# Three tiles multiplied while x comes in, first weight pieces from two queues, and state additions issued later than their products

## The chip, the cores and the metric

The kernel runs on one core of a Trainium2 chip. The metric is device time in microseconds, from the first to the last instruction of the core with what the launch adds around it; lower is better.

## What is computed

One inference step of a hybrid layer, in float32: 256 prompt tokens and 8 x 8 sample tokens (320 columns, T) share the weights. One input projection (2048 to 13344 columns) feeds a Mamba-2 SSD mixer and a gated short convolution, and one output projection takes both. The reference, cut:

```python
h = rmsnorm(x, norm_w)
proj = jnp.einsum('bld,de->ble', h, w_in)
z_s, xbc, dt_raw, z_c, b_c, c_c, v_c = jnp.split(proj, SPLIT_POINTS, axis=-1)
xbc, buf_ssd_new = causal_dwconv(xbc, buf_ssd, conv_ssd_w)      # width 4
xbc = jax.nn.silu(xbc + conv_ssd_b)
xs, bm, cm = jnp.split(xbc, (D_SSM, D_SSM + SSD_GN), axis=-1)
dt = jax.nn.softplus(dt_raw + dt_bias)
y_s, h_new = ssd_scan(xs, dt, -jnp.exp(a_log), bm, cm, d_skip, h_ssm)  # h_new = h * decay + B (dt x)
y_s = grouped_rmsnorm(y_s * jax.nn.silu(z_s), ssd_norm_w, SSD_GROUPS)
conv_out, buf_short_new = causal_dwconv(c_c * v_c, buf_short, conv_short_w)
y_c = b_c * conv_out * jax.nn.silu(z_c)
y = jnp.einsum('ble,ed->bld', jnp.concatenate([y_s, y_c], axis=-1), w_out)
return x + y, h_new, buf_ssd_new, buf_short_new
```

The 8 samples each carry an SSD state of 32 heads x 64 x 128 in and out.

## The kernel before

The input projection is cut into tiles of 128 output columns; `schedule()` lists them: B, C, dt, four x and four z tiles of SSD group 0, four tiles of the short convolution, then the same for groups 1 to 3, then the other short convolutions. A tile is 16 pieces of 128 x 128 weights (k = 0 to 15) against `x`, which lies with its 2048 features over 16 pieces of 128 partitions x 320 columns. To keep float32 accuracy at the faster fp32r rate, weights and x are split: ScalarE casts a quarter tile (`wh`, L145), VectorE subtracts for the rest (`wl`, L146), and each piece takes three products, L165 to L167 (L245 to L247 for the first two tiles). The dt tile has its rest in spare columns and takes two (L161, L162). x is scaled by the norm weight and split the same way into `xh` (ScalarE, L235) and `xl` (VectorE, L236). The row norm itself is computed beside the first products and multiplied in behind the projection (`rb`, L307): it needs the squares of x (L239 on POOL for three quarters, L241 on ScalarE for the last), their sums (L250, L251) and two small groups of products (`rstd`, L260 and L277).

Weights come on SyncE's queue (SP, L132) into three buffers of half a tile; `wh` and `wl` have six buffers of a quarter each, so the split of the next tile runs up to one and a half tiles ahead of the products. Tiles 0 and 1 are multiplied piece by piece as x arrives; tile 2 (dt) follows from its own loads, with `rstd` advanced between its pieces, and tiles 3 onward run in the loop at L691. There, `advance(1)` at three pieces of each tile (`TICKS`) lets a generator issue its next step: `decays()` first (the steps of dt, `laT`, `tr1` and so on), then `ssd_group(g)` for each group. A step ends at a `yield`.

Of `ssd_group`, the change touches the samples' states (L539 to L562). For q = 0 and 1, four states `ht` (b = 2j + q) are multiplied with C (`py`, L542), the four updates `up` come from eight products (L548), POOL multiplies each state with its decay (L552), VectorE adds the update (L554), and POOL stores the state (L555). Behind that come the decay matrices `R` (loaded at L461, steps at L585, exp at L588, product with CBm at L589) and `CE` (L577 on ScalarE, L578 on POOL).

The code's order is not the order on the engines: a scheduler in the framework places each instruction by its own estimate. The order below is read from the built kernels.

Of the kernel before, what the change touches and what calls it, by code (L numbers as in the profile page):

```python
# [84 lines left out]
def hymba_step(ctx: ExitStack, tc: tile.TileContext, A, O):  # L85
# [34 lines left out]
    def load(i):  # L120
# [12 lines left out]
            got.append(r)  # L133
        raws[i] = got

    def split_quarter(i, q):
# [2 lines left out]
        if i < nin and tiles[i][0] == "dt":

            S.copy(h, r)
            V.tensor_sub(h[:, :, H:2 * H], r[:, :, H:2 * H], h[:, :, H:2 * H].bitcast(F32))
            return h, None
# [4 lines left out]

    def split(i):
        if i >= NTILE or i in splits:  # L150
            return
        load(i)
        splits[i] = [split_quarter(i, q) for q in range(KT // KQ)]

    def product(ps, i, hi, lo, start=True, stop=True, tick=None, ticks=TICKS):
        for k in range(KT):
            if tick and k in ticks:
                tick()
            h, l = splits[i][k // KQ]
            if l is None:  # L160
                PE.matmul(ps, h[:, k % KQ, :], hi(k), start=k == 0, stop=False)  # L161
                PE.matmul(ps, h[:, k % KQ, :], lo(k), start=False, stop=k == KT - 1)  # L162
                continue
# [63 lines left out]
    ps0 = [psj.tile([P, T], F32, name=f"pj{i}", tag="pj") for i in range(2)]  # L227
    for q in range(KT // KQ):
        ks = slice(q * KQ, (q + 1) * KQ)
        wq = []  # L230
        for i in range(2):
            wq.append(split_quarter(i, q))
        for k in range(q * KQ, (q + 1) * KQ):
            nwk = vec[:, V_NW + k:V_NW + k + 1]
            S.activation(xh[:, k, :], xr[:, k, :], AF.Copy, scale=nwk)  # L235
            V.scalar_tensor_tensor(out=xl[:, k, :], in0=xr[:, k, :], scalar=nwk,  # L236
                                   in1=xh[:, k, :].bitcast(F32), op0=ALU.mult, op1=ALU.subtract)
        if q < 3:
            GP.tensor_tensor(out=sqx[q], in0=xr[:, ks, :], in1=xr[:, ks, :], op=ALU.mult)  # L239
        else:  # L240
            S.activation(sqx[q], xr[:, ks, :], AF.Square)  # L241
        for k in range(q * KQ, (q + 1) * KQ):
            for i in range(2):
                h, l = wq[i][0][:, k % KQ, :], wq[i][1][:, k % KQ, :]
                PE.matmul(ps0[i], h, xh[:, k, :], start=k == 0, stop=False)  # L245
                PE.matmul(ps0[i], l, xh[:, k, :], start=False, stop=False)  # L246
                PE.matmul(ps0[i], h, xl[:, k, :], start=False, stop=k == KT - 1)  # L247
    acc = sqx[0]
    for q in range(1, 4):
        V.tensor_tensor(out=acc, in0=acc, in1=sqx[q], op=ALU.add)  # L250
# [27 lines left out]
        out.append(p2[:, :T])  # L278

    def inproj(i):  # L280
        if tiles[i][0] == "dt":
            ps = pss.tile([P, 512], F32, name="pdt", tag="py", bufs=1)[:, :T]
        else:
            ps = psj.tile([P, T], F32, name=f"pj{i}", tag="pj")
# [589 lines left out]
```

## Time and profile before

| | us |
|---|---|
| median of 3 runs | 1061.34 (1057.29 to 1063.15) |
| the profiled execution | 1064.92 |
| its span, first to last instruction | 1063.1 |
| TensorE busy in it | 1032.8 |
| VectorE, ScalarE, POOL busy in it | 667.2, 484.5, 193.3 |

Times in the profile are us from the span's start. PE is TensorE's products, PEld its weight loads, DVE VectorE, ACT ScalarE, POOL GpSimd, SP SyncE; L12 is line 12 of the kernel, and a line may be that of a helper, so that L146 is every rest of a split. A product's duration contains its way through the array, so the distance of two starts is its cost in a row of products. The granted clock is the share of TensorE's full 2.4 GHz; its two levels read as 1.00 and 0.50. The profile prints 1.00 from the start of the span, also where products are spaced as at the low level.

### The profile page before, as it was taken

The page shows a single profiled execution, that of the slowest core. Times are in us where ns is not written, and L with a number is a line of the kernel's source. Part 1 is how long each engine was busy: PE and PEld are TensorE (multiplying, and loading weights), DVE is VectorE, ACT ScalarE, POOL GpSimd, SP SyncE. Part 2 cuts the span into 40 slices and gives each one's busy share as a digit, 9 for nine tenths or more (in the row PEclk, how much of TensorE's full clock was granted, in tenths as well). Part 3 has the DMA queues.
Part 4 walks back from the last instruction along what each step waited for, and adds up shares of the span by engine and source line. Part 5 has one row for each costly group of instructions (what it writes and reads, how often), then busy time and mean ns, then how long its engine had stood idle before and what let it go on. Part 6 is the DMA issues. An engine that isn't in the chain of part 4 may idle for free.

```text
span 1063.1 us, 18415 instructions
## 1 busy us (share of the span) xinstructions
PE 1032.8 (97%) x7110; PEld 1006.8 (95%) x7110; DVE 667.2 (63%) x1202; ACT 484.5 (46%) x850; POOL 193.3 (18%) x276
## 2 busy tenths in 40 slices
PE   6999999999999999999999999999999999999995
PEld 5989899989998999889999999999999999999994
DVE  7776878688867976697555555555555644444443
ACT  6663456435654455355444344444444544444440
POOL 3322422062104411342111111111111000000000
PEclk8999999999999999999999999999999999999997
DMA  7446645575448545754745545454545445454542
GB/s 265 145 140 219 199 138 159 163 244 186 141 139 278 178 141 170 253 183 154 244 144 154 149 149 154 145 158 142 156 144 160 146 152 152 146 155 144 157 120 99
DMA packets 64119, 177.18 MB, mean 167 GB/s; under 512 B 10672, under 2 KB 19888, under 8 KB 63904
## 3 DMA queue, kind: packets, MB, share of 16 engines
q1 hardware_dynamic: 60848, 166.04, 50.2%
q0 software_dynamic: 3040, 9.96, 2.5%
q8 instruction: 55, 0.90, 0.4%
q14 instruction: 32, 0.26, 0.1%
q10 hardware_dynamic: 144, 0.01, 0.0%
HBM read 163.41 MB, written 12.58 MB: 166 GB/s over the span
## 4 chain that ended last, share of the span: by engine, by line
PE 89%; DVE 5%; DMA 3%; issue 1%; ACT 1%; POOL 0%; SPq 0%; DVEq 0%; ACTq 0%; POOLq 0%
PE pj L165 21%; PE pj L166 21%; PE pj L167 20%; PE po L167 7%; PE po L165 7%; PE po L166 7%; DVE wl L146 2%; DMA wr<-in_w_in 1%; PE pd L601 1%; DVE ht L554 1%; PE st L528 1%; DVE res L784 1%; DMA xr<-in_x 1%; DMA R<-acd 0%; PE pj L246 0%
## 5 line engine op out<-in xcount | busy, mean ns | idle before, releaser
L146 DVE TENSOR_TENSOR wl<-wr,wh 128x512 fp32r<-128x512 f32 x544 | 386.8, 716 | 299.4 <-ACT wh L145 295.2
L145 ACT CAST wh<-wr 128x512 fp32r<-128x512 f32 x544 | 333.0, 619 | 460.2 <-PE pj L167 309.1
L165 PE MATMUL pj<-xh,wh 128*128 128x320 f32 x1632 | 513.0, 314 | 0.0
L166 PE MATMUL pj<-xh,wl 128*128 128x320 f32 x1632 | 505.2, 310 | 6.6 <-DVE wl L146 6.6
L167 PE MATMUL pj<-xl,wh 128*128 128x320 f32 x1632 | 504.2, 309 | 0.0
L166 PEld LDWEIGHTS pj<-xh,wl 128*128 128x128 f32 x1632 | 306.8, 188 | 10.3 <-DVE wl L146 7.9
L165 PEld LDWEIGHTS pj<-xh,wh 128*128 128x128 f32 x1632 | 306.7, 188 | 6.4 <-issue 4.8
L167 PEld LDWEIGHTS pj<-xl,wh 128*128 128x128 f32 x1632 | 306.8, 188 | 0.0
L167 PE MATMUL po<-ycl,wh 128*128 128x320 f32 x256 | 79.0, 309 | 0.0
L166 PE MATMUL po<-ysh,wl 128*128 128x320 f32 x256 | 79.0, 309 | 0.0
L166 PE MATMUL po<-ych,wl 128*128 128x320 f32 x256 | 79.0, 309 | 0.0
L165 PE MATMUL po<-ych,wh 128*128 128x320 f32 x256 | 79.0, 309 | 0.0
L165 PE MATMUL po<-ysh,wh 128*128 128x320 f32 x256 | 79.0, 309 | 0.0
L167 PE MATMUL po<-ysl,wh 128*128 128x320 f32 x256 | 79.0, 308 | 0.0
L657 POOL COPY sso<-pad 128x18 f32<-128x18 f32 x16 | 5.1, 316 | 237.2 <-DVE pad L655 237.2
L166 PEld LDWEIGHTS po<-ych,wl 128*128 128x128 f32 x256 | 48.0, 187 | 0.0
L165 PEld LDWEIGHTS po<-ysh,wh 128*128 128x128 f32 x256 | 48.0, 187 | 0.0
L166 PEld LDWEIGHTS po<-ysh,wl 128*128 128x128 f32 x256 | 48.0, 187 | 0.0
L165 PEld LDWEIGHTS po<-ych,wh 128*128 128x128 f32 x256 | 48.0, 187 | 0.0
L167 PEld LDWEIGHTS po<-ycl,wh 128*128 128x128 f32 x256 | 48.0, 187 | 0.0
L167 PEld LDWEIGHTS po<-ysl,wh 128*128 128x128 f32 x256 | 48.0, 187 | 0.0
L765 POOL TENSOR_TENSOR acco<-acco,sqo 128x320 f32<-128x320 f32 x13 | 11.7, 899 | 190.9 <-ACT sqo L764 190.9
(213 smaller groups left out, 847.4 us busy)
## 6 DMA issues: line engine op xcount, KB each, us to landing
wr<-in_w_in SPq DMA_DIRECT2D x206, 512.0 KB, 3.7
wr<-in_w_out SPq DMA_DIRECT2D x64, 512.0 KB, 3.8
ht<-in_h SPq DMA_DIRECT2D x32, 256.0 KB, 5.9
out_hs<-ht POOLq DMA_DIRECT2D x32, 256.0 KB, 4.6
R<-acd SPq DMA_DIRECT2D x20, 256.0 KB, 6.9
res<-in_x SPq DMA_DIRECT2D x1, 2560.0 KB, 9.9
xr<-in_x SPq DMA_DIRECT2D x7, 320.0 KB, 6.3
wr<-in_w_in SPq DMA_DIRECT2D x8, 256.0 KB, 6.2
```

What stands on the lines that cost most here:

```text
L145: S.copy(h, r)
L146: V.tensor_sub(l, r, h.bitcast(F32))
L165: PE.matmul(ps, h, hi(k), start=start and k == 0, stop=False)
L166: PE.matmul(ps, l, hi(k), start=False, stop=False)
L167: PE.matmul(ps, h, lo(k), start=False, stop=stop and k == KT - 1)
L528: PE.matmul(p, Btok[:, c * P:(c + 1) * P], xw, start=True, stop=True)
L554: V.tensor_tensor(out=ht, in0=ht, in1=ups[j], op=ALU.add)
L601: PE.matmul(pd[u * HD:(u + 1) * HD, o:o + n], xdt[c][:, h * HD:(h + 1) * HD], Rs[c, h][0][:, Rs[c, h][1], :], start=True, stop=c != 1)
L657: GP.tensor_copy(sso[:, j], win(pad, TP, (NL + 2, NB + 1), (1, 2)))
L765: GP.tensor_tensor(out=acc, in0=acc, in1=sq, op=ALU.add)
L784: V.tensor_tensor(out=r[:, d, :], in0=r[:, d, :], in1=pr[0], op=ALU.mult)
```

## The change

Start. Tiles 0, 1 and 2 (`NFIRST` = 3, dt among them) are multiplied piece by piece as x arrives. Their first quarter is loaded in pieces of two k instead of four, the first such piece of tiles 0 and 2 from ScalarE's queue, all else from SP. Ten products of a zero tile (`NWARM`) stand ahead of the first real product. The accumulators of the three tiles lie in other PSUM pools than before, all squares of x are ScalarE's, and `rstd` is advanced between the pieces of tile 4 (`NFIRST` + 1). Tiles 3 and 4 are multiplied ahead of the loop and kept in `ahead`; the convolutions of tiles 0, 1, 3 and 4 follow when `rb` is there.

States. In `ssd_group` the loads of the odd states are issued before the `up` products, POOL's four multiplications are issued together, and the additions and stores follow behind a `yield`, two and two with another `yield` between them. The two yields that followed for q = 0 stay. A group thus has three steps more.

The diff, cut to its core:

```diff
-    for q in range(KT // KQ):
-        for k in range(q * KQ, (q + 1) * KQ, 2):
-            if k:
-                SP.dma_start(xr[:, k:k + 2, :], A["x"][:, k:k + 2, :])
-            if k == q * KQ:
-                for i in range(2):
-                    SP.dma_start(raws[i][k // KH][:, k % KH:k % KH + KQ, :], A["w_in"][i, :, k:k + KQ, :])
...
+    xload(0, 1)
     S.dma_start(vec[:, :KT], A["vec"][:, :KT])
+    first(S, 0, 0, 2)
+    first(SP, 1, 0, 2)
+    first(S, 2, 0, 2)
+    xload(1, 1)
+    for i in range(NFIRST):
+        first(SP, i, 2, 2)
+    xload(2, 2)
+    for q in range(1, KT // KQ):
+        for i in range(NFIRST):
+            first(SP, i, q * KQ, KQ)
+        xload(q * KQ, 2)
+        xload(q * KQ + 2, 2)
...
+    psw = psj.tile([P, T], F32, name="pjw", tag="pj")
+    for _ in range(NWARM):
+        PE.matmul(psw[:, :P], warm, warm, start=True, stop=True)
...
+    for q in range(KT // KQ):
+        k0 = q * KQ
+        wq = [wtiles(i, q) for i in range(NFIRST)]
+        n = 2 if q == 0 else KQ
+        for k in range(0, KQ, n):
+            for i in range(NFIRST):
+                if i == 0 and n == 2:
+                    xsplit(k0 + k)
+                split_piece(i, wq[i], k0 + k, n)
+            for m in range(n == 2, n):
+                xsplit(k0 + k + m)
+            for kk in range(k0 + k, k0 + k + n):
+                for i in range(NFIRST):
+                    h, l = wq[i]
+                    PE.matmul(ps0[i], h[:, kk % KQ, :], xh[:, kk, :], start=kk == 0, stop=False)
+                    if l is not None:
+                        PE.matmul(ps0[i], l[:, kk % KQ, :], xh[:, kk, :], start=False, stop=False)
+                    PE.matmul(ps0[i], h[:, kk % KQ, :], xl[:, kk, :], start=False, stop=kk == KT - 1)
+    split(3)
+    load(4)
...
-        if q < 3:
-            GP.tensor_tensor(out=sqx[q], in0=xr[:, ks, :], in1=xr[:, ks, :], op=ALU.mult)
-        else:
-            S.activation(sqx[q], xr[:, ks, :], AF.Square)
...
+    for q in range(4):
+        S.activation(sqx[q], xr[:, q * KQ:(q + 1) * KQ, :], AF.Square)
...
+    ahead = {}
     pr = []
-    gens.append(rstd([acc[:, n, :] for n in range(2)], DM, "rx", pr))
-    pdt = inproj(2)
+    for i in range(NFIRST, NFIRST + 2):
+        load(i + 2)
+        split(i + 1)
+        if i == NFIRST + 1:
+            gens.append(rstd([acc[:, n, :] for n in range(2)], DM, "rx", pr))
+        ahead[i] = inproj(i)
...
+            if q == 0:
+                for b in range(4):
+                    hload(2 * b + 1)
             ups = [sm(f"up{g}_{q}_{j}") for j in range(4)]
...
-                ht = hts.pop(b)
+                ht = hts[b]
                 GP.tensor_tensor(out=heads(ht, g), in0=heads(ht, g),
                                  in1=perhead(dec[:, b * H + HPG * g:b * H + HPG * (g + 1)]), op=ALU.mult)
+            yield
+            for j in range(4):
+                b = 2 * j + q
+                ht = hts.pop(b)
                 V.tensor_tensor(out=ht, in0=ht, in1=ups[j], op=ALU.add)
                 GP.dma_start(O["hs"][g, :, b, :], ht)
+                if j == 1:
+                    yield
             if q == 0:
-                for b in range(4):
-                    hload(2 * b + 1)
-                yield
                 yield
                 yield
```

What stands in a row on the engines, at the places that the prediction speaks of. `wh0_1` is quarter 1 of tile 0, the last number an instance. ScalarE at the second quarter of the first tiles, before:

```order
L235 ACTIVATE xh_75<-xr_80,vec_81 128x320 x4
L145 CAST wh0_1_182<-wr0_0_84 128x512
L145 CAST wh1_1_186<-wr1_0_86 128x512
L235 ACTIVATE xh_75<-xr_80,vec_81 128x320 x4
L145 CAST wh0_2_223<-wr0_1_85 128x512
L145 CAST wh1_2_227<-wr1_1_87 128x512
```

and now:

```order
L253 ACTIVATE xh_75<-xr_80,vec_83 128x320 x2
L144 CAST wh0_1_213<-wr0_0_84 128x512
L285 ACTIVATE sqx0_386<-xr_80 128x1280
L144 CAST wh1_1_215<-wr1_0_86 128x512
L144 CAST wh2_1_217<-wr2_0_88 128x512
L253 ACTIVATE xh_75<-xr_80,vec_83 128x320 x4
L144 CAST wh0_2_264<-wr0_1_85 128x512
L144 CAST wh1_2_266<-wr1_1_87 128x512
L285 ACTIVATE sqx1_387<-xr_80 128x1280
```

There are three casts instead of two for each quarter, and a square of x stands among them. 

VectorE in the second half of the states of group 1, before (`wl26_3` is the last rest of tile 26, `wl27_0` the first of tile 27, `c1` a product of the short convolution):

```order
L146 TENSOR_TENSOR wl26_3_2592<-wr26_1_2462,wh26_3_2591 128x512
L562 TENSOR_TENSOR xdt2_1_2344<-xdt2_1_2344,py1_2517 128x512
L589 TENSOR_TENSOR R2_0_1_2655<-R2_0_1_2655,CBm1_2317 128x512
L554 TENSOR_TENSOR ht1_1_2546<-ht1_1_2546,up1_1_0_2630 128x512
L554 TENSOR_TENSOR ht3_1_2548<-ht3_1_2548,up1_1_1_2631 128x512
L554 TENSOR_TENSOR ht5_1_2550<-ht5_1_2550,up1_1_2_2632 128x512
L554 TENSOR_TENSOR ht7_1_2552<-ht7_1_2552,up1_1_3_2633 128x512
L146 TENSOR_TENSOR wl27_0_2684<-wr27_0_2575,wh27_0_2683 128x512
L647 TENSOR_TENSOR c1_2677<-pj25_2595,rb2_397 128x320
```

and now:

```order
L149 TENSOR_TENSOR wl26_3_2612<-wr26_1_2486,wh26_3_2611 128x512
L633 TENSOR_TENSOR R2_0_1_2750<-R2_0_1_2750,CBm1_2341 128x512
L633 TENSOR_TENSOR R0_0_1_2752<-R0_0_1_2752,CBm1_2341 128x512
L149 TENSOR_TENSOR wl27_0_2695<-wr27_0_2595,wh27_0_2694 128x512
L633 TENSOR_TENSOR R0_1_1_2816<-R0_1_1_2816,CBm1_2341 128x512
L606 TENSOR_TENSOR xdt2_1_2368<-xdt2_1_2368,py1_2541 128x512
L629 TENSOR_SCALAR R1_0_1_2843<-R1_0_1_2843,ac_tok_569 128x128
L599 TENSOR_TENSOR ht1_1_2546<-ht1_1_2546,up1_1_0_2669 128x512
L599 TENSOR_TENSOR ht3_1_2548<-ht3_1_2548,up1_1_1_2670 128x512
L691 TENSOR_TENSOR c1_2688<-pj25_2615,rb2_559 128x320
L149 TENSOR_TENSOR wl27_1_2699<-wr27_0_2595,wh27_1_2698 128x512
L599 TENSOR_TENSOR ht5_1_2550<-ht5_1_2550,up1_1_2_2671 128x512
```

The additions to ht1 and ht3 moved behind `wl27_0`, those to ht5 and ht7 behind `wl27_1`; the R products moved ahead of them.

VectorE in the first half of the same group now:

```order
L149 TENSOR_TENSOR wl25_3_2501<-wr25_1_2384,wh25_3_2500 128x512
L599 TENSOR_TENSOR ht0_1_2443<-ht0_1_2443,up1_0_0_2554 128x512
L599 TENSOR_TENSOR ht2_1_2445<-ht2_1_2445,up1_0_1_2555 128x512
L599 TENSOR_TENSOR ht4_1_2447<-ht4_1_2447,up1_0_2_2556 128x512
L599 TENSOR_TENSOR ht6_1_2449<-ht6_1_2449,up1_0_3_2557 128x512
L149 TENSOR_TENSOR wl26_0_2600<-wr26_0_2484,wh26_0_2599 128x512
```

The same six rows stood there before, in this order.

POOL in the second half of group 1, before:

```order
L578 TENSOR_TENSOR CE0_1_2820<-CE0_1_2820,C1_1841 128x512
L552 TENSOR_TENSOR ht1_1_2546<-ht1_1_2546,dec_408 128x512
L552 TENSOR_TENSOR ht3_1_2548<-ht3_1_2548,dec_408 128x512
L552 TENSOR_TENSOR ht5_1_2550<-ht5_1_2550,dec_408 128x512
L552 TENSOR_TENSOR ht7_1_2552<-ht7_1_2552,dec_408 128x512
L578 TENSOR_TENSOR CE1_1_2844<-CE1_1_2844,C1_1841 128x512
L555 DMA out_hs<-ht1_1_2546 128x512
```

and now:

```order
L622 TENSOR_TENSOR CE0_1_2919<-CE0_1_2919,C1_1858 128x512
L622 TENSOR_TENSOR CE1_1_2943<-CE1_1_2943,C1_1858 128x512
L593 TENSOR_TENSOR ht1_1_2546<-ht1_1_2546,dec_570 128x512
L593 TENSOR_TENSOR ht3_1_2548<-ht3_1_2548,dec_570 128x512
L593 TENSOR_TENSOR ht5_1_2550<-ht5_1_2550,dec_570 128x512
L593 TENSOR_TENSOR ht7_1_2552<-ht7_1_2552,dec_570 128x512
L600 DMA out_hs<-ht1_1_2546 128x512
```

The second CE product moved ahead of the four multiplications. On SP the loads of the odd states keep their place among the weights.

## Rows read from the trace of the kernel before

**Rows 1.** The page, busy time of each engine: us busy, share of the span, instructions.

```profile
PE 1032.8 (97%) x7110; PEld 1006.8 (95%) x7110; DVE 667.2 (63%) x1202; ACT 484.5 (46%) x850; POOL 193.3 (18%) x276
```

**Rows 2.** The table of stretches, all engines; a line gives the stretch and its length, then busy us (and instructions) of PE, PEld, DVE, ACT and POOL, the granted TensorE clock, the DMA share and GB/s.

```profile
0.00:5.57 5.57, 0.00 (x1) 0.01 (x1) 0.57 (x2) 2.71 (x5) 0.44 (x9) 1.00 0.63 162
5.57:18.00 12.43, 8.71 (x29) 6.81 (x29) 11.23 (x10) 10.54 (x22) 7.68 (x3) 0.95 1.01 375
18.00:24.00 6.00, 6.00 (x24) 6.00 (x25) 6.00 (x11) 2.51 (x4) 0.00 (x0) 0.54 0.66 246
...
90.00:130.00 40.00, 37.61 (x243) 33.25 (x243) 30.24 (x61) 15.00 (x26) 17.94 (x20) 0.96 0.72 237
...
200.00:245.00 45.00, 43.29 (x296) 39.19 (x295) 35.64 (x69) 18.10 (x31) 17.81 (x21) 1.00 0.68 223
...
300.00:355.00 55.00, 54.67 (x377) 50.56 (x376) 41.31 (x81) 23.08 (x42) 19.02 (x24) 1.00 0.69 216
...
410.00:470.00 60.00, 57.80 (x398) 53.69 (x398) 44.44 (x84) 25.32 (x47) 19.40 (x26) 1.00 0.64 208
```

**Rows 3.** The timeline of TensorE, from the first product to the first products of tile 3 (37.15); start, us, engine, line, operation, output<-input, in brackets the idle time before it and what ended it.

```profile
5.57 0.64 PE L245 MATMUL pj<-xh,wh 128*128 128x320 f32 x1 [5.57 <-ACT wh L145]
...
12.57 0.47 PE L246 MATMUL pj<-xh,wl 128*128 128x320 f32 x1
12.84 0.47 PE L247 MATMUL pj<-xl,wh 128*128 128x320 f32 x1
...
17.87 0.64 PE L246 MATMUL pj<-xh,wl 128*128 128x320 f32 x1 [2.02 <-DVE wl L146]
...
32.51 1.39 PE L260 MATMUL rxs<-ones,sqx 128*128 128x1 f32 x12
33.76 0.39 PE L161 MATMUL pdt<-xh,wh 128*128 128x320 f32 x1
...
36.19 0.83 PE L277 MATMUL rxb<-con,rxr 128*128 128x128 f32 x6
36.78 0.39 PE L161 MATMUL pdt<-xh,wh 128*128 128x320 f32 x1
...
37.15 0.31 PE L165 MATMUL pj<-xh,wh 128*128 128x320 f32 x1
37.30 0.31 PE L166 MATMUL pj<-xh,wl 128*128 128x320 f32 x1
```

**Rows 4.** The table of stretches of 1 us for TensorE alone, behind the idle spell of group 0: busy us, granted clock, DMA share, GB/s.

```profile
126.00:127.00 1.00, 1.00 (x6) 0.50 1.07 270
129.00:130.00 1.00, 1.00 (x7) 0.86 0.04 8
```

**Rows 5.** The timelines of ScalarE, VectorE and POOL while x comes in, columns as in rows 3.

```profile
8.00 1.92 ACT L235 ACTIVATE xh<-xr,vec 128x320 fp32r<-128x320 f32 x4 [0.24 <-DMA xr<-in_x]
9.82 1.12 ACT L145 CAST wh<-wr 128x512 fp32r<-128x512 f32 x2
...
17.32 1.01 ACT L235 ACTIVATE xh<-xr,vec 128x320 fp32r<-128x320 f32 x2
18.24 1.26 ACT L241 ACTIVATE sqx<-xr 128x1280 f32<-128x1280 f32 x1
...
8.60 5.89 DVE L236 SCALAR_TENSOR_TENSOR xl<-xr,vec,xh 128x320 fp32r<-128x320 f32 x4
...
8.14 2.53 POOL L239 TENSOR_TENSOR sqx<-xr 128x1280 f32<-128x1280 f32 x1 [7.17 <-DMA xr<-in_x]
```

**Rows 6.** The list of DMA issues of the first 20 us: output<-input, queue, count, KB each, median us from issue to landing.

```profile
xr<-in_x SPq DMA_DIRECT2D x7, 320.0 KB, 6.3
wr<-in_w_in SPq DMA_DIRECT2D x8, 256.0 KB, 6.2
...
xr<-in_x SPq DMA_DIRECT2D x2, 160.0 KB, 3.0
```

**Rows 7.** The list of waits, TensorE: who waited for whom, us in total, times, longest.

```profile
PE pj L166 <- DVE wl L146: 6.6, 5, 2.2
...
PE tr L377 <- DVE laT L370: 1.3, 1, 1.3
```

**Rows 8.** The timelines of VectorE and POOL in group 2, behind ScalarE's first CE (341.36), and of TensorE at the wait of group 0 (124.43), columns as in rows 3.

```profile
341.36 2.53 DVE L585 TENSOR_SCALAR R<-R,ac_tok 128x128 f32<-128x128 f32 x3 [0.66 <-ACT CE L577]
343.82 3.00 DVE L146 TENSOR_TENSOR wl<-wr,wh 128x512 fp32r<-128x512 f32 x2
346.74 0.68 DVE L562 TENSOR_TENSOR xdt<-xdt,py 128x512 f32<-128x512 f32 x1
...
348.19 2.47 DVE L554 TENSOR_TENSOR ht<-ht,up 128x512 f32<-128x512 f32 x4
350.58 0.68 DVE L146 TENSOR_TENSOR wl<-wr,wh 128x512 fp32r<-128x512 f32 x1
...
342.77 4.95 POOL L552 TENSOR_TENSOR ht<-ht,dec 128x512 f32<-128x512 f32 x4
...
124.43 0.41 PE L166 MATMUL pj<-xh,wl 128*128 128x320 f32 x1 [2.11 <-DVE wl L146]
```

**Rows 9.** The timeline of VectorE at the first two convolutions, six steps.

```profile
40.71 3.01 DVE L437 SCALAR_TENSOR_TENSOR cv<-pad,vec,cv 128x344 f32<-128x344 f32 x6
```

**Rows 10.** The view of one tile, R, from 100 to 125 us (group 0): duration in ns, min/median/max, first and last start.

```profile
L585 DVE TENSOR_SCALAR R<-R,ac_tok x19: 249/282/1328, 107.5 to 115.9; 128x128 f32<-128x128 f32 x11, 128x64 f32<-128x64 f32 x8
```

More of the change, by code (lines that the diff above doesn't have):

```diff
@@ L69 @@
 TICKS = (5, 10, 15)
+NFIRST = 3
+NWARM = 10
 def schedule():
@@ L134, in load, with split_piece @@
         raws[i] = got
+    def split_piece(i, hl, k, n):
+        r = raws[i][k // KH][:, k % KH:k % KH + n, :]
+        h, l = hl
+        h = h[:, k % KQ:k % KQ + n, :]
+        S.copy(h, r)
+        if l is None:
+            V.tensor_sub(h[:, :, H:2 * H], r[:, :, H:2 * H], h[:, :, H:2 * H].bitcast(F32))
+        else:
+            V.tensor_sub(l[:, k % KQ:k % KQ + n, :], r, h.bitcast(F32))
     def split_quarter(i, q):
-        r = raws[i][q * KQ // KH][:, (q * KQ) % KH:(q * KQ) % KH + KQ, :]
         h = wp.tile([P, KQ, P], F32R, name=f"wh{i}_{q}", tag="wh", bufs=6)
[L139 to L143, printed above, removed]
         l = wp.tile([P, KQ, P], F32R, name=f"wl{i}_{q}", tag="wl", bufs=6)
-        S.copy(h, r)
-        V.tensor_sub(l, r, h.bitcast(F32))
+        split_piece(i, (h, l), q * KQ, KQ)
         return h, l
@@ L159, in product @@
             h, l = splits[i][k // KQ]
[L160 to L163, printed above, removed]
             h, l = h[:, k % KQ, :], l[:, k % KQ, :]
@@ L173, in hymba_step, with first, xload @@
     xr = sp0.tile([P, KT, T], F32, name="xr")
+    warm = sp0.tile([P, P], F32, name="warm")
+    V.memset(warm, 0.0)
     vec = cp.tile([P, NV], F32, name="vec")
-    SP.dma_start(xr[:, :1, :], A["x"][:, :1, :])
-    S.dma_start(vec[:, :KT], A["vec"][:, :KT])
-    for i in range(2):
-        raws[i] = [sp0.tile([P, KH, P], F32, name=f"wr{i}_{hf}") for hf in range(2)]
-    for q in range(KT // KQ):
-        for k in range(q * KQ, (q + 1) * KQ, 2):
-            if k:
-                SP.dma_start(xr[:, k:k + 2, :], A["x"][:, k:k + 2, :])
-            if k == q * KQ:
-                for i in range(2):
-                    SP.dma_start(raws[i][k // KH][:, k % KH:k % KH + KQ, :], A["w_in"][i, :, k:k + KQ, :])
-                    if i == k == 0:
-                        SP.dma_start(xr[:, 1:2, :], A["x"][:, 1:2, :])
-    load(2)
+    for i in range(NFIRST):
+        raws[i] = [sp0.tile([P, KH, P], F32, name=f"wr{i}_{hf}") for hf in range(2)]
+    def first(e, i, k, n):
+        e.dma_start(raws[i][k // KH][:, k % KH:k % KH + n, :], A["w_in"][i, :, k:k + n, :])
+    def xload(k, n):
+        SP.dma_start(xr[:, k:k + n, :], A["x"][:, k:k + n, :])
+    xload(0, 1)
+    S.dma_start(vec[:, :KT], A["vec"][:, :KT])
+    first(S, 0, 0, 2)
[10 more added lines that the diff above has]
+        xload(q * KQ + 2, 2)
     con = cp.tile([P, NC_], F32, name="con")
@@ new lines, in hymba_step, with xsplit @@
+    psw = psj.tile([P, T], F32, name="pjw", tag="pj")
+    for _ in range(NWARM):
+        PE.matmul(psw[:, :P], warm, warm, start=True, stop=True)
+    ps0 = [sm(f"pf{i}")[:, :T] for i in range(2)]
+    ps0.append(pss.tile([P, 512], F32, name="pdt", tag="py", bufs=1)[:, :T])
+    pdt = ps0[2]
+    def xsplit(k):
+        nwk = vec[:, V_NW + k:V_NW + k + 1]
+        S.activation(xh[:, k, :], xr[:, k, :], AF.Copy, scale=nwk)
+        V.scalar_tensor_tensor(out=xl[:, k, :], in0=xr[:, k, :], scalar=nwk,
+                               in1=xh[:, k, :].bitcast(F32), op0=ALU.mult, op1=ALU.subtract)
@@ new lines, in wtiles @@
+    def wtiles(i, q):
+        h = wp.tile([P, KQ, P], F32R, name=f"wh{i}_{q}", tag="wh", bufs=6)
+        if tiles[i][0] == "dt":
+            return h, None
+        return h, wp.tile([P, KQ, P], F32R, name=f"wl{i}_{q}", tag="wl", bufs=6)
+    for q in range(KT // KQ):
[10 more added lines that the diff above has]
+            for kk in range(k0 + k, k0 + k + n):
+                for i in range(NFIRST):
+                    h, l = wq[i]
[3 more added lines that the diff above has]
+                    PE.matmul(ps0[i], h[:, kk % KQ, :], xl[:, kk, :], start=False, stop=kk == KT - 1)
@@ L280, in inproj @@
     def inproj(i):
[L281 to L284, printed above, removed]
+        ps = psj.tile([P, T], F32, name=f"pj{i}", tag="pj")
         product(ps, i, lambda k: xh[:, k, :], lambda k: xl[:, k, :], tick=lambda: advance(1))
@@ L694, in hymba_step @@
             ps = ps0[i]
+        elif i in ahead:
+            ps = ahead.pop(i)
         else:
```

20 lines of the change are left out of this document (removed).

## The prediction

> **What bounds the kernel now.** I read the page's busy table first: TensorE is busy for 1032.8 us of a span of 1063.1 [rows 1]. So an edit is worth only TensorE time without a product, or products at the low clock; the reader is to look for these two and for nothing else. The table of stretches gives the idle time: 5.57 us before the first product, 12.43 - 8.71 = 3.72 us while x comes in, and 2.39, 1.71, 0.33 and 2.20 us in the stretches that hold the four SSD groups [rows 2]. The rest lies at the kernel's end, which the change does not touch. The timeline of TensorE gives the clock. Warm, products of 320 columns start 0.146 us apart (37.15 to 37.30); at 12.57 to 12.84 they are still 0.27 us apart, which is the lower level, 1.2 of 2.4 GHz [rows 3]. From 18 to 24 us only 24 products run, granted 0.54 [rows 2]. Behind the idle spell of group 0 the grant is 0.50 until about 129 us, with 6 products a us [rows 4]. The list of waits names who is late: in the groups the rest of a split weight piece (`wl`) from VectorE, 6.6 us in five waits, and once 1.3 us for `laT` [rows 7].
>
> **First tiles.** Before, tiles 0 and 1 take their 96 products while x comes, and the 32 of dt follow; tile 3 begins at 37.15. In between lie the row-norm products, 33.76 - 32.51 = 1.25 and 36.78 - 36.19 = 0.59 us [rows 3], which now move behind tile 3. The same 128 products thus end at the equivalent of 37.15 - 1.84 = 35.3 us.
> Now for the new end. *Transfers.* Ahead of x pieces 2 and 3 stood 160 + 256 + 160 + 256 KB, with themselves 1152 KB, and ScalarE went on at 8.00 when they had landed [rows 5, 6]. Now it is two times 160, six of 128 and 320 = 1408 KB. The 256 KB more cost 0.7 us at 375 GB/s or 1.6 us at 162 [rows 2]; I take 0.9, so 8.9. *ScalarE.* Its pieces follow each other 0.46 us apart for x (1.92 for four), 0.5 for a cast (1.12 for two), 1.2 for a square [rows 5]. Between the landing and x piece 4 stand two x, three casts and a square, which the order puts there: 0.9 + 1.5 + 1.2, so piece 4 is ready at 13.1. *TensorE.* Behind it are 12 of 16 pieces with 8 products each, 96 x 0.146 = 14.0, hence 27.1. *Who else could be last:* ScalarE has 14 x, 9 casts and 3 squares from 8.9 on, 6.4 + 4.5 + 3.6, and ends at 23.4. VectorE has about as much, now without POOL's squares beside it, with which four x rests took 5.89 us [rows 5]. The last x came at 17.3 [rows 5]; 1 MB more at 375 GB/s makes it 20.1. So TensorE itself is last. I add 0.9 us for spells at the low clock, since it still waits at about 6 to 9 and 11.6 to 13 us: tile 3 begins at 28.0, **a gain of 7.3**. Bounds: without the square in the way 25.9 (9.4 gained). With two spells like that of 18 to 24 us, where 24 products took 6.0 instead of 3.5 us [rows 2, 3], it is 32.1 (3.2 gained).
> The ten warming products read 128 columns. Two row-norm products of this shape start some 0.2 us apart warm [rows 3]; at the low level twice that, 4 us in all, so they end near 5.2 where the first real one starts at 5.57 now. They can hold up only the first pieces, which then wait for x 2 and 3 anyway: nothing. The two pieces on ScalarE's queue I count at nothing too: what they bring early waits likewise.
> **The burst behind.** Four convolutions instead of two now follow the row norm. Between `rb` and the first weight rest of tile 7 VectorE has some 13 us to do: twelve convolution steps alone are 6.0 [rows 9]. TensorE has tiles 5 and 6 to cover it, 96 x 0.146 = 14.0. It fits with 0.9 us to spare; if it does not, the excess is a wait. The wait of 1.3 us for `laT` [rows 7] moves into tile 8 and I leave it as it is, with 1 us to either side.
>
> **State additions.** The first half of each group does not change its place: in the order of VectorE the four additions of ht0, 2, 4 and 6 still stand in one piece. The second half does. Take group 2. From the end of ScalarE's CE at 341.36 VectorE does three R, two `wl`, xdt, R, four additions, and then the first rest of the next tile, ready at 351.2 [rows 8]. An addition is 0.6 us, a rest 0.6 (0.68 with its tail), an R product with CBm 0.65 alone. Now (group 1 in the order, tiles 26 and 27) only two R products stand between `wl26_3` and `wl27_0`, so piece 0 is early by more than the wait. But an R product, xdt, an R step, two additions and c come before `wl27_1`. Counted up to piece 1, the queue holds two R products and a short step more and two additions less: 1.3 + 0.2 - 1.2 = 0.3 us more than before. TensorE needs piece 1 one quarter tile, 12 x 0.146 = 1.75 us, after piece 0. Before, c and a rest, 1.0 us, lay between them. So a wait of w at piece 0 becomes w + 1.0 + 0.3 - 1.75 = w - 0.45 at piece 1. The waits of 2.11 [rows 8], 1.71, 0.33 and 2.20 (group 0 had 0.28 more, earlier) turn into 1.7, 1.25, 0 and 1.75: the work is mostly moved. That is 1.9 us. POOL's multiplications now stand behind CE1, so the two rests at 343.82, 3.00 us beside them [rows 8] where two take 1.3, lose their neighbour and others get it. I take 0.6 us for that. The low spell after group 0 (about 3.4 us, so 1.6 lost [rows 4]) may go with the shorter wait: 0.5. **Gain 3.0**; bounds -1 (a little more contention) and 8.2 (all waits and the spell gone). On POOL the stores queue behind the additions as they did; POOL is busy for 18% [rows 1]. The early odd loads keep their place in SP's order.
>
> **Rivals.** *The clock falls again.* While TensorE waits for x, the grant drops as it did for 18 to 24 us, and two slow spells take 5 us: 3.2 in place of 7.3, so 1056.9. For it: products of 8.9 to 13 us leave gaps. Against it: the longest gap then is about 2 us, and the drop came behind two waits, the second of 2.02 us [rows 3]. The Trainium skill, page "TensorE: Matmul & The Clock Gate", section "What's actually happening", has the low clock as the default that activity releases; by that the ten products help and the gaps hurt, and the trace agrees on both.
> *The group waits go altogether.* If the moved multiplications fall beside operations that read PSUM, VectorE is not stretched: 6.6 + 1.6 instead of 3.0, so 1047.6. For it: beside POOL's work xdt took 0.68 [rows 8]. Against it: the count above.
> *POOL's port, slower.* The moved multiplications stand beside R, R, `wl`, R, which read SBUF twice. In group 2, three R steps (0.28 each by their median [rows 10]) and two rests would take 2.2 alone and took 5.4: a stretch of 3.2 us beside POOL work of 6.3 us. If the whole 6.3 counted in the new place, each group would lose 3.1 more, 12.4 in all, and a wait that long brings the low spell that 2.11 us brought to group 0, 1.6 us in each: 1063.1 - 10.3 + 12.4 + 6.4 = 1071.6. It decides from 10.3 / 4 = 2.6 us of added loss in each group. Against it: the old neighbours read SBUF alone too. The Trainium skill, page "SBUF — State Buffer", section "SBUF: two separate sides", calls the port an exclusive lock for the whole instruction; by it the full stretch would be paid, and the trace shows half.
>
> **The numbers.** The profiled execution took 1064.92 us, the median is 1061.34 (1057.29 to 1063.15). Its products are the same in each run, so a faster run has less waiting to lose; I start from the middle of the two, 1063.1. 1063.1 - 7.3 - 3.0 = 1052.8: **1053 us**. Chances: the forecast (1050 to 1056) 0.55; the clock 0.17; group waits all gone 0.13; both halves bring little (about 1060) 0.10; slower by the port 0.05. A measurement of this kernel tells about 0.5% (5.3 us) from no change, so faster begins below 1056.0: 0.55, 0.13 and part of the clock case, 0.75; the same 0.20; slower 0.05. The range, 1046 to 1059, holds the first three cases.
>
> **What would show it.** Right: first product of tile 3 near 28 us; 0.146 us spacing from 13 us on; no square on POOL; idle of 1 to 2 us before the second piece of tiles 13, 27 and 55 and none before the first. Wrong: tile 3 after 31 us or a grant of 0.5 beyond 15 us (clock); rests of 1.5 us in a row and waits over 3 us in the groups (port); a wait before tile 7 (burst); no waits in the groups.

## The result and the profile after

The changed kernel takes 1047.78 us (median of 4 runs, 1047.37 to 1048.97); the kernel before took 1062.24 (1057.29 to 1064.19) beside it. The ratio is 0.9873, 95% interval 0.9837 to 0.9908: faster by 14.5 us, where 10 were forecast. The time lies in the stated range, but outside the 1050 to 1056 of the likeliest case; it is where the second rival (the group waits go altogether, 1047.6) had put it.

The page, busy time of each engine, against [rows 1]:

```profile
PE 1028.9 (98%) x7130; PEld 1004.4 (96%) x7130; DVE 656.2 (63%) x1206; ACT 486.7 (47%) x856; POOL 188.1 (18%) x273
```

The span is 1045.6 us, 17.5 less than that of the profiled execution before. That execution was slower than its kernel's median (1064.92 us against 1062.24), the one after slightly faster than its own, so 3 of the 17.5 us are scatter between executions; where in the kernel they lie no trace shows. TensorE's busy time fell by 3.9 only, so most of the rest is idle time that is gone. The list of waits, TensorE (who waited for whom, us in total, times, longest), of the changed kernel, against [rows 7]:

```profile
PE pf L277 <- ACT xh L253: 1.3, 2, 0.9
...
PE pjw L245 <- DVE warm L180: 1.1, 1, 1.1
PE pdt L277 <- DVE wh L147: 0.6, 1, 0.6
PE tr L415 <- DVE laT L408: 0.4, 1, 0.4
```

No line for `wl` is left: neither the 3.2 us while x came in nor the 6.6 us of the groups. Where the 17.5 us came from is read from two tiles whose place in the order is the same in both kernels: the transposes `xt`, ahead of the state work in each group, and the output products `po` behind all groups. The view of one tile, first of the kernel before, then of the changed one; the times are the first and the last start:

```profile
L516 PE MATMUL xt<-con,x x32: 271/272/273, 89.1 to 436.4; 128*128 128x128 f32 x32
L165 PE MATMUL po<-ych,wh x256: 307/308/310, 822.2 to 1040.0; 128*128 128x320 f32 x128
```

```profile
L554 PE MATMUL xt<-con,x x32: 270/272/273, 80.3 to 421.0; 128*128 128x128 f32 x32
L169 PE MATMUL po<-ych,wh x256: 310/310/310, 804.5 to 1022.3; 128*128 128x320 f32 x128
```

At the first `xt` the changed kernel is 89.1 - 80.3 = 8.8 us ahead, at the first `po` 822.2 - 804.5 = 17.7. So between these two executions the stretch up to the first `xt` gave 8.8 us and the four groups 8.9. The start itself, timeline of TensorE, against [rows 3]:

```profile
1.06 4.37 PE L245 MATMUL pjw<-warm 128*128 128x128 f32 x20 [1.06 <-DVE warm L180]
5.18 0.54 PE L277 MATMUL pf<-xh,wh 128*128 128x320 f32 x2
5.57 0.31 PE L279 MATMUL pf<-xh,wl 128*128 128x320 f32 x1
5.71 0.31 PE L280 MATMUL pf<-xl,wh 128*128 128x320 f32 x1
...
12.97 0.42 PE L277 MATMUL pf<-xh,wh 128*128 128x320 f32 x1 [0.87 <-ACT xh L253]
...
27.48 0.31 PE L169 MATMUL pj<-xh,wh 128*128 128x320 f32 x1
```

Products in a row are 0.146 us apart (the upper level, 2.4 GHz) from 5.57 on, the last gap is the one before x piece 4, at 12.97, and tile 3 begins at 27.48 where 28.0 was forecast. Group 2, timelines of VectorE and then POOL behind ScalarE's first CE (which ends at about 326.0), against [rows 8]:

```profile
323.27 4.54 DVE L629 TENSOR_SCALAR R<-R,ac_tok 128x64 f32<-128x64 f32 x17
327.74 1.28 DVE L149 TENSOR_TENSOR wl<-wr,wh 128x512 fp32r<-128x512 f32 x2
...
333.62 0.69 DVE L599 TENSOR_TENSOR ht<-ht,up 128x512 f32<-128x512 f32 x1 [0.96 <-POOL ht L593]
334.63 0.69 DVE L599 TENSOR_TENSOR ht<-ht,up 128x512 f32<-128x512 f32 x1 [0.32 <-POOL ht L593]
335.23 0.48 DVE L691 TENSOR_TENSOR c<-pj,rb 128x320 f32<-128x320 f32 x1
335.63 1.52 DVE L149 TENSOR_TENSOR wl<-wr,wh 128x512 fp32r<-128x512 f32 x1
337.07 1.27 DVE L599 TENSOR_TENSOR ht<-ht,up 128x512 f32<-128x512 f32 x2
```

```profile
326.05 1.29 POOL L622 TENSOR_TENSOR CE<-CE,C 128x512 f32<-128x512 f32 x1 [3.18 <-ACT CE L621]
329.69 2.90 POOL L622 TENSOR_TENSOR CE<-CE,C 128x512 f32<-128x512 f32 x1 [2.35 <-ACT CE L621]
332.54 4.06 POOL L593 TENSOR_TENSOR ht<-ht,dec 128x512 f32<-128x512 f32 x4
```

Two rests that took 3.00 us now take 1.28, since POOL's multiplications start at 332.54, behind them. The price stands further down: the additions wait for POOL, 0.96 and 0.32 us, and the rest of piece 1 of tile 41 takes 1.52 beside it. It is ready at 337.07. TensorE starts tile 41 at 335.88 and needs the piece for its 14th product, 335.88 + 13 x 0.146 = 337.78: 0.7 us to spare. Behind the other three groups nothing is to spare. In group 0 the rest of piece 1 of tile 13 starts at 113.15 and ends at 113.15 + 1.52 = 114.67; its product starts at 114.72, 0.33 us behind the one before instead of 0.146. Such a delay is too short to show in the list of waits.

### The profile page after: what moved, and what is told of

Read it like the earlier page. It is cut to its first block, busy times and chain, and to the rows that moved or that the text cites. A ratio compares the mean times of both kernels' runs of the same rounds, so it can differ in the third digit from the quotient of the medians.

```text
span 1045.6 us, 18464 instructions
## 1 busy us (share of the span) xinstructions
PE 1028.9 (98%) x7130; PEld 1004.4 (96%) x7130; DVE 656.2 (63%) x1206; ACT 486.7 (47%) x856; POOL 188.1 (18%) x273
## 4 chain that ended last, share of the span: by engine, by line
PE 95%; DVE 3%; ACT 1%; DMA 1%; issue 0%; DVEq 0%; SPq 0%
PE pj L169 23%; PE pj L170 22%; PE pj L171 22%; PE po L169 7%; PE po L171 7%; PE po L170 7%; PE pd L645 1%; PE py L580 1%; DVE cv L475 1%; PE st L566 1%; DVE res L830 1%; PE up L589 1%; DVE wl L149 0%; DMA xr<-in_x 0%; ACT xh L253 0%
## 5 line engine op out<-in xcount | busy, mean ns | idle before, releaser
L149 DVE TENSOR_TENSOR wl<-wr,wh 128x512 fp32r<-128x512 f32 (+1 forms) x546 | 385.1, 711 | 297.0 <-ACT wh L144 293.3
L144 ACT CAST wh<-wr 128x512 fp32r<-128x512 f32 (+1 forms) x551 | 334.8, 616 | 441.9 <-PE pj L171 282.7
```

The source lines that it names most:

```text
L149: V.tensor_sub(l[:, k % KQ:k % KQ + n, :], r, h.bitcast(F32))
```

## The experiments

Times are medians; "before" is the kernel before, run beside the others, and ratios stand with their 95% interval.

**The two halves by themselves.** `start_only` has the changed start and ssd_group() as before, `groups_only` the other way round.

> The new start with the state updates of the kernel before. Theory (the two halves are independent): tile 3 begins at 27.5 as in the changed kernel, and the group waits come back: about 6 us of idle time for wl, some 9 us on the path with the low clock behind the longest; 1055 to 1058. Rival (the new start alone removes the waits, because VectorE's order in front of the group changes too): under 2 us of waits for wl, 1047 to 1050.

> The start of the kernel before with the new state updates. Theory (independent halves): tile 3 begins at 37.2, no wait for wl in the groups; 1054 to 1057. Rival (the groups gain only with the new start): waits for wl of 3 us or more remain, 1058 to 1062.

Before took 1064.48 us. `start_only`: 1051.94, ratio 0.9889 (0.9863 to 0.9915). `groups_only`: 1057.24, 0.9934 (0.9912 to 0.9956). Alone they gain 12.5 and 7.2 us, 19.8 in sum, against 14.5 for both at once (at a median of 1062.24 us before). Their lists of waits, TensorE, `start_only` first:

```profile
PE pj L170 <- DVE wl L149: 3.3, 3, 1.7
```

```profile
PE pj L166 <- DVE wl L146: 1.5, 3, 0.8
```

With the old state updates and the new start the group waits come back, but only half of them, 3.3 of 6.6 us. Neither expectation had that. With the new updates and the old start 1.5 us are left, between the two expectations as well. So the halves overlap: each takes away part of the same waits. The first starts of `xt` and `po` say how much, since the four groups lie between them:

| kernel | first `xt` | first `po` | between |
|---|---|---|---|
| before | 89.1 | 822.2 | 733.1 |
| before, profiled again | 90.0 | 822.8 | 732.8 |
| start_only | 79.9 | 807.8 | 727.9 |
| groups_only | 88.3 | 814.5 | 726.2 |
| the changed kernel | 80.3 | 804.5 | 724.2 |

The new start alone takes 5.2 us off the groups, the new updates alone 6.9, both together 8.9. On top of the new start the updates are thus worth 3.7 us. The seven profiles of variants of the start further down, with the new updates, have 723.5 to 724.8 between the two tiles.

**POOL's work or the place of the additions?** `no_odd_mult` is `start_only` without POOL's second four multiplications, so it leaves the decay of the odd samples' states out:

```diff
-                GP.tensor_tensor(out=heads(ht, g), in0=heads(ht, g), ...
+                if q == 0:
+                    GP.tensor_tensor(out=heads(ht, g), in0=heads(ht, g), ...
```

> As start_only, with the additions of the second half in one piece at their old place, but POOL's four multiplications of the second half are left out (the odd sequences' states are not decayed). Theory A (what the move took away is POOL's work beside VectorE: the last R steps 3.4 us and the two rests 3.0 us beside it): R steps at 1.8 or less and two rests in 1.3, VectorE 2.3 to 3.3 us earlier in each group, no wait or under 1 us in all; 1047 to 1049. Theory B (of the forecast: what counts is that the additions stand behind a piece of the next tile, POOL's company is worth 0.6 us in all): four additions of 0.6 us stay ahead of the first piece and waits of 4 us or more remain; 1052 to 1056.

1047.07 us, ratio 0.9848 (0.9826 to 0.9871), and no wait for `wl` at all, with all four additions still in one piece ahead of the next tile. Theory A holds. From the first `xt` (80.5) to the first `po` (803.9) it takes 723.4 us, 0.8 less than the changed kernel. Group 2 of `start_only`, VectorE and POOL behind the first CE, and then of `no_odd_mult`:

```profile
326.40 3.44 DVE L623 TENSOR_SCALAR R<-R,ac_tok 128x128 f32<-128x128 f32 x3 [0.25 <-ACT CE L615]
329.76 3.00 DVE L149 TENSOR_TENSOR wl<-wr,wh 128x512 fp32r<-128x512 f32 x2
326.45 1.30 POOL L616 TENSOR_TENSOR CE<-CE,C 128x512 f32<-128x512 f32 x1 [3.32 <-ACT CE L615]
327.70 4.50 POOL L590 TENSOR_TENSOR ht<-ht,dec 128x512 f32<-128x512 f32 x4
```

```profile
322.95 4.44 DVE L624 TENSOR_SCALAR R<-R,ac_tok 128x64 f32<-128x64 f32 x17
327.31 1.28 DVE L149 TENSOR_TENSOR wl<-wr,wh 128x512 fp32r<-128x512 f32 x2
...
325.62 1.28 POOL L617 TENSOR_TENSOR CE<-CE,C 128x512 f32<-128x512 f32 x1 [3.07 <-ACT CE L616]
328.74 1.30 POOL L617 TENSOR_TENSOR CE<-CE,C 128x512 f32<-128x512 f32 x1 [1.83 <-ACT CE L616]
```

In `start_only` five VectorE operations, worth 3 x 0.28 + 2 x 0.6 = 2.0 us alone [rows 8, 10], last from 326.40 to 332.68, about as long as the five POOL operations beside them (326.45 to 332.20). Instruction by instruction they take turns: the three R end at 327.83, 328.84 and 329.84, each 0.08 us behind the end of a POOL operation (327.75, 328.75, 329.76). The Trainium skill, page "SBUF — State Buffer", section "SBUF: two separate sides", has the port as an exclusive lock for a whole instruction; these rows agree, 6.3 us for 2.0.

**Is it enough to come later?** `late_one_piece` is the changed kernel with multiplication and addition in one loop again. The two yields of that loop stand behind the first half instead, so that the second half comes as late as in the changed kernel:

```diff
-            yield
-            for j in range(4):
-                b = 2 * j + q
-                ht = hts.pop(b)
                 V.tensor_tensor(out=ht, in0=ht, in1=ups[j], op=ALU.add)
                 GP.dma_start(O["hs"][g, :, b, :], ht)
-                if j == 1:
-                    yield
             if q == 0:
+                yield
+                yield
```

> As the changed kernel, POOL's second half behind both CE, but the four additions in one piece again, ahead of the second piece of the next tile. In the changed kernel that piece was ready within 0.3 us of its need. Theory (splitting two and two matters, since VectorE waits for POOL's multiplications, one in 1.0 us): the second piece is about 1 us late in each group, 3 to 5 us of waits, 1050 to 1053. Rival (only the later POOL place matters): under 1 us of waits, 1047 to 1049.

1051.53 us, ratio 0.9885 (0.9858 to 0.9913), as slow as `start_only`. The theory holds. Its wait line, and VectorE in group 2:

```profile
PE pj L170 <- DVE wl L149: 4.3, 4, 1.4
```

```profile
335.84 0.69 DVE L595 TENSOR_TENSOR ht<-ht,up 128x512 f32<-128x512 f32 x1 [0.95 <-POOL ht L593]
...
338.85 0.69 DVE L595 TENSOR_TENSOR ht<-ht,up 128x512 f32<-128x512 f32 x1 [0.31 <-POOL ht L593]
339.45 0.48 DVE L687 TENSOR_TENSOR c<-pj,rb 128x320 f32<-128x320 f32 x1
339.85 1.28 DVE L149 TENSOR_TENSOR wl<-wr,wh 128x512 fp32r<-128x512 f32 x2
```

VectorE is free of POOL in front, but then waits for it at each of four additions, all ahead of piece 1. So moving POOL's work paid nothing without parting the additions. The additions parted with POOL's work in its old place were not run.

**The parts of the start.** Before took 1063.40 us beside these four; in each, the state updates are the new ones, so the start of tile 3 tells the part's worth. In profiles with the changed kernel's start it was 27.00 to 27.66.

`no_warm` leaves the ten warming products out (and their tile and memset).

> The changed kernel without the ten warming products. Theory of the forecast (they are worth nothing, since the first 32 products wait for x pieces 2 and 3 anyway): tile 3 at 27 to 28, time within 1 us of the changed kernel, 1047 to 1049. Rival (the first products then run at the low clock, 0.27 us apart instead of 0.146, until about 13 us, and the waits do not hide all of it): the 32nd product near 14 instead of 12, tile 3 at 28.5 to 30, 1048.5 to 1051; if the gaps bring the low clock back later, 31 or more.

`squares_on_pool` gives three squares of x back to POOL:

```diff
+        if q < 3:
+            GP.tensor_tensor(out=sqx[q], in0=xq, in1=xq, op=ALU.mult)
+        else:
+            S.activation(sqx[q], xq, AF.Square)
```

> The changed kernel with three of the four squares of x on POOL again, as before. Theory (POOL's squares beside VectorE were what held the start back: four x rests took 5.9 us beside one, 1.9 alone): VectorE loses 3 to 4 us in each of two quarters against 1.2 us that ScalarE gains, waits for xl or wl of 1 to 4 us, tile 3 at 29 to 32, 1049 to 1053. Rival (ScalarE is the last one, so each square taken off it gives time): tile 3 at 26.5, 1046 to 1047.

`big_pieces` has first weight pieces of 256 KB, all on SP's queue:

```diff
-    first(S, 0, 0, 2)
-    first(SP, 1, 0, 2)
-    first(S, 2, 0, 2)
+    for i in range(NFIRST):
+        first(SP, i, 0, KQ)
```

> The changed kernel with first weight pieces of 256 KB, all on SP's queue, casts and rests of a whole quarter. Theory of the forecast (small pieces and the second queue bring nothing, what they bring early waits for x): first real product near 6, tile 3 at 27 to 28.5, 1047 to 1049. Rival (the first 768 KB ahead of x hold the start up): first product at 6.5 or later, x pieces 2 and 3 split after 10, tile 3 at 29 to 30.5, 1049 to 1051.

`two_tiles` sets NFIRST to 2 and multiplies dt behind tiles 0 and 1, as before.

> The changed kernel with two tiles while x comes in; dt follows them, ahead of tile 3. Theory (the third tile gives TensorE work where it would wait for ScalarE, whose quarter takes 2 casts, 4 x and a square, 4.2 us, against 24 products or 3.5 us): waits of some 0.7 us a quarter more, tile 3 at 28 to 30, 1048 to 1050. Rival (the third tile matters little, TensorE is never short by then and the gain is from the clock and the squares): tile 3 at 26.5 to 27.7, 1046 to 1048. If the third tile were the whole gain, tile 3 would come near 33 to 35 and the time near 1054.

| kernel | us | ratio to before | tile 3 at |
|---|---|---|---|
| no_warm | 1047.93 | 0.9853 (0.9827 to 0.9880) | 27.30 |
| squares_on_pool | 1052.23 | 0.9892 (0.9865 to 0.9919) | 32.73 |
| big_pieces | 1047.11 | 0.9848 (0.9822 to 0.9874) | 27.95 |
| two_tiles | 1049.10 | 0.9878 (0.9842 to 0.9914) | 28.86 |

The warming products and the small pieces (with the second queue) are worth nothing that can be measured. By the start of tile 3 the third tile is worth 1.4 us and the squares on ScalarE 5.2 us, most of the start; by the medians against the changed kernel's 1047.78 us the two are 1.3 and 4.5. `squares_on_pool`, timelines of VectorE and POOL:

```profile
9.09 2.58 DVE L254 SCALAR_TENSOR_TENSOR xl<-xr,vec,xh 128x320 fp32r<-128x320 f32 x2 [0.69 <-ACT xh L253]
...
12.99 3.99 DVE L254 SCALAR_TENSOR_TENSOR xl<-xr,vec,xh 128x320 fp32r<-128x320 f32 x4
...
18.31 3.41 DVE L149 TENSOR_TENSOR wl<-wr,wh 128x512 fp32r<-128x512 f32 x2
...
8.54 2.32 POOL L287 TENSOR_TENSOR sqx<-xr 128x1280 f32<-128x1280 f32 x1 [7.56 <-DMA xr<-in_x]
13.31 2.41 POOL L287 TENSOR_TENSOR sqx<-xr 128x1280 f32<-128x1280 f32 x1 [2.45 <-DMA xr<-in_x]
17.00 3.57 POOL L287 TENSOR_TENSOR sqx<-xr 128x1280 f32<-128x1280 f32 x1 [1.29 <-DMA xr<-in_x]
```

Each square stops VectorE for 1.6 to 2.1 us: 2.58 where two x rests take 1.01 in the changed kernel (from 9.32), 3.99 where four take 1.94 (12.95), 3.41 where two weight rests take 1.29 (14.82). In `no_warm` the first products are slow, as its rival said, and yet nothing is lost. Timeline of TensorE:

```profile
8.14 0.47 PE L274 MATMUL pf<-xh,wl 128*128 128x320 f32 x1
8.41 0.47 PE L275 MATMUL pf<-xl,wh 128*128 128x320 f32 x1
8.68 0.37 PE L272 MATMUL pf<-xh,wh 128*128 128x320 f32 x1
8.89 0.31 PE L274 MATMUL pf<-xh,wl 128*128 128x320 f32 x1
9.04 0.31 PE L275 MATMUL pf<-xl,wh 128*128 128x320 f32 x1
...
12.77 0.41 PE L272 MATMUL pf<-xh,wh 128*128 128x320 f32 x1 [0.79 <-ACT xh L248]
```

They are 0.27 us apart until 8.7, the lower level, then 0.146; the gap ahead of x piece 4 at 12.77 swallows the loss.

**A better version?** `sq_late` holds the squares back with a scale of 1 made from the last rest of x; `x_first` issues two x pieces of a quarter ahead of its weights; `x_first_late` does both.

```diff
+    V.tensor_scalar(out=one, in0=xl[:, KT - 1, 0:1].bitcast(F32), scalar1=0.0, scalar2=1.0, op0=ALU.mult, op1=ALU.add)
-        S.activation(sqx[q], xr[:, q * KQ:(q + 1) * KQ, :], AF.Square)
+        S.activation(sqx[q], xr[:, q * KQ:(q + 1) * KQ, :], AF.Square, scale=one[:, 0:1])
```

```diff
+        xload(q * KQ, 2)
         for i in range(NFIRST):
             first(SP, i, q * KQ, KQ)
-        xload(q * KQ, 2)
```

> The changed kernel with the squares of x held back until the last rest of x (a scale of 1 that is made behind it; ScalarE's order then has no square among the x pieces). Theory of the forecast (the square ahead of x piece 4 holds it up; bound without it 25.9): x piece 4 at 11.2 to 11.7, no gap before the 33rd product, tile 3 at 26 to 26.7, 1046 to 1047. Rival (x piece 4 lands only then, the square hides in that wait, as squares_on_pool shows, where ScalarE waits for x until 12.4 without a square ahead): x piece 4 at 12.2 to 12.5, tile 3 at 27 to 27.7, 1047 to 1048; the later row norm could cost up to 1 us more.

> The changed kernel with the first two x pieces of each later quarter issued ahead of its three weight pieces. Theory (the landing of x piece 4 is what the 33rd product waits for): x piece 4 up to 0.7 us earlier with the square still ahead of the casts, the first cast last instead; tile 3 at 26.6 to 27.3, 1046.5 to 1047.5. Rival (ScalarE's own queue sets it): unchanged, 27.3 to 27.7.

> Both edits together: x pieces ahead of the weights, squares behind the last rest of x. If landing and ScalarE's queue each hold the 33rd product up to the same moment, only both together gain: 33rd product near 12.0, tile 3 at 26.2 to 26.6, 1046 to 1047. If something else is last (the weight pieces), as sq_late.

Before took 1064.58 us. 1046.84, 1047.21 and 1047.01 us; ratios 0.9830 (0.9806 to 0.9853), 0.9833 (0.9815 to 0.9851), 0.9833 (0.9817 to 0.9848); tile 3 at 26.89, 27.55 and 26.26. Only both edits together close the gap ahead of x piece 4 (landing and ScalarE's queue hold it up to nearly the same moment), and that gives 1.2 us in the trace and nothing that the times can tell.

**The kernel before once more.** It was profiled again, for the overlap of the halves.

> The kernel before, unchanged, profiled once more. The two halves alone gained 12.5 and 7.2 us, together more than both at once, since the waits for wl in the groups fell from 6.6 to 3.3 us with the new start alone. Theory (how late the R loads land differs from run to run, so the profiled execution of before had more to lose than another one): the first CE's table load at other times behind tile 11, 25, 39 and 53 than 7.0, 4.9, 4.7 and 5.8 us, and group waits of another sum, 2 to 7 us, with the span following them. Rival (the old start itself makes the R loads late): the four times again near 5.6 in the mean and waits of 6 us or more.

1061.45 us against 1062.05, ratio 0.9991 (0.9976 to 1.0006). The time that counts is when ScalarE's exp table load starts, behind the last R load; here in group 0 of the kernel before and of the changed one, timeline of ScalarE:

```profile
112.51 1.28 ACT L577 ACT_TABLE_LOAD   x1 [3.84 <-DMA R<-acd]
```

```profile
102.17 1.28 ACT L621 ACT_TABLE_LOAD   x1 [1.80 <-DMA R<-acd]
```

Counted from the first product of tile 11, that is 7.00 and 5.49 us. The four groups have 7.00, 4.90, 4.67 and 5.38 in the first profile of before (the 5.8 of the expectation is too high) and 5.49, 4.70, 4.11 and 4.78 in that of the changed kernel. In the new profile of before they have 6.25, 5.86, 4.25 and 5.37 (mean 5.4), with 6.4 us of waits, none of them in the group with 4.25. So single groups scatter by up to 1 us, as the theory has it, and the mean and the sum stay, as the rival has it. Over the three profiles with the old start the mean is 5.40 (12 groups), over the eleven with the new start 4.81 (44 groups). The rival is the better one.

## Why the prediction held, and where not

- **What bounds the kernel.** Right: all that was gained is idle time of TensorE and products at the low clock.
- **First tiles.** Right in size and reason: 35.3 - 27.48 = 7.8 us gained where 7.3 were forecast. x pieces 2 and 3 let ScalarE go on at 8.7 (forecast 8.9), the product for piece 4 started at 12.97 (piece ready at 13.1), then TensorE ran without a gap worth naming. The 0.9 us for the low clock was not needed; small delays took 0.5 of it (12.97 + 96 x 0.146 = 27.0, measured 27.48). `squares_on_pool` shows which edit carried it. The lower bound of 25.9, without the square in the way, was not reached by taking only the square away (26.89); x piece 4 lands hardly earlier.
- **Warming products, two queues, small pieces at nothing.** Right, `no_warm` and `big_pieces`, and for the reason given: what comes early waits for x.
- **The burst behind.** It fitted: no wait ahead of tile 7. The wait for `laT` fell from 1.3 to 0.4 us instead of staying, inside the 1 us allowed; with the 7.8 this makes the 8.8 at the first `xt`.
- **State additions.** The step that failed is the size of the gain in the groups: 3.0 us forecast, 8.9 between the two profiled executions (by the medians 14.5 - 8.8 = 5.7 would be left for them). Two terms were mis-sized. The forecast gave the new start no effect on the groups, and alone it took 5.2 us off them; on top of it the updates brought 3.7. And "the work is mostly moved" (w becomes w - 0.45) was wrong, with 0.6 us too little for the lost neighbour. Group 3 shows the second. Rows of VectorE, kernel before, then the changed one:

```profile
454.08 3.44 DVE L585 TENSOR_SCALAR R<-R,ac_tok 128x128 f32<-128x128 f32 x3 [1.38 <-ACT CE L577]
457.45 3.00 DVE L146 TENSOR_TENSOR wl<-wr,wh 128x512 fp32r<-128x512 f32 x2
...
464.47 0.68 DVE L146 TENSOR_TENSOR wl<-wr,wh 128x512 fp32r<-128x512 f32 x1
```

```profile
438.05 1.81 DVE L629 TENSOR_SCALAR R<-R,ac_tok 128x128 f32<-128x128 f32 x3 [0.77 <-ACT CE L621]
439.78 1.28 DVE L149 TENSOR_TENSOR wl<-wr,wh 128x512 fp32r<-128x512 f32 x2
...
447.68 1.52 DVE L149 TENSOR_TENSOR wl<-wr,wh 128x512 fp32r<-128x512 f32 x1
```

From CE to the end of piece 0 it was 464.47 + 0.60 - 454.08 = 11.0 us; from CE to the end of piece 1 it is now 447.68 + 1.44 - 438.05 = 11.1, and piece 1 is needed 1.75 later. So 1.7 us are gained in this group, not 0.45. In front POOL's absence saves 1.6 + 1.7 = 3.3 us; behind, waiting for POOL and the rest beside it give back some 2.1. Done in the same way, groups 0 to 2 gain 1.1, 1.7 and 0.5: 5.0 in all against 4 x 0.45 + 0.6 = 2.4 by the forecast's two terms.
- **What the forecast did not have.** CE comes earlier in all four groups, by 1.5, 0.2, 0.6 and 0.6 us, 2.9 in all. `start_only` has 3.0 at the same places, so it goes with the start. Why the R loads land earlier with the new start stays open. Together with the 5.0 this is 7.9 us, more than the 6.6 us of waits, so the waits went. The products at the low clock behind the wait of group 0 went too: from tile 11 to tile 22 that group took 194.26 - 105.51 = 88.75 us and now takes 181.32 - 96.68 = 84.64. Of these 4.1 us 2.39 were idle before; of the other 1.7, 0.5 had been counted.
- **The rivals.** The clock did not fall: behind gaps of up to 0.87 us the granted clock from 13 to 28 us is 1.00. The slower port did not come: POOL's new neighbours do wait for it, but piece 0 is done before them and piece 1 comes just in time. The prediction had read the trace as half of what an exclusive lock would cost; the turns in `start_only` show the whole of it, one POOL operation for each VectorE operation. The second rival came true, and with it the sign "no waits in the groups". Its reason is half right: VectorE's operations in front are no longer stretched; in the new place one still is (1.52). That the time lies 0.2 us from this rival's 1047.6 is partly luck: the rival has 7.3 us for the start and 8.2 for the groups, the traces have 8.8 and 8.9, and it started from 1063.1 where the median beside the changed kernel was 1062.24.

## What to carry to other kernels

Price work on POOL by what stands beside it on VectorE, operation for operation: a POOL that is busy for 18% cost this kernel 5 us at the start, and VectorE 2 to 3 us in each group. When an operation is moved away from such a neighbour, look where it lands: the later place paid only because the additions that wait for POOL were parted around the piece that TensorE needs. Two edits that shorten the same waits do not add up, even where they stand far apart in the program; measure each alone before crediting either.

## What the runs showed of the hardware beyond what was expected

When VectorE and POOL clash, either may be the one that waits. In `start_only` VectorE does (five operations in 6.3 us instead of 2.0). In the changed kernel POOL does: its second CE, 1.30 us in `no_odd_mult`, takes 2.90 from 329.69 on, while VectorE's R product, rest and R product there take their usual 0.6 us each. It ends at 332.59, so 1.30 us of work would begin at 331.29, just where VectorE turns from these (two inputs from SBUF) to `xdt` (one from PSUM). In `no_warm` the clock rose to the upper level behind eleven slow products in a row, at 8.7 us, and was still there after the 0.8 us gap ahead of x piece 4. And a wait of some 2 us may or may not bring the lower level. In the profile of before 2.11 us in group 0 brought it, and 2.20 us in group 3 did not (products 0.146 us apart right behind it). In its second profile 2.34 us in group 1 brought it, and 1.92 and 2.19 us in groups 0 and 3 did not. So 1.6 us of slow products for every long wait, as the port's rival had it, is too much.
